# A two-branch recurrent encoder with 32 experts: single-input work goes from VectorE to ScalarE, and the router and the end are rearranged

## The chip, the cores and the metric

The kernel runs on one core of a Trainium2 chip. The metric is the device time of one execution in microseconds (us). Before the change it is 1595.73 us, the median of three runs (1595.01 to 1598.45).

## The reference, cut to what matters

One layer works on 256 tokens of width 1024, in float32.

```
p = x @ w_in                                   # 1024 x 10560
o_a = hgrn2(p...)      # 8 heads, gated linear attention, both directions, chunks
o_b = rwkv7(p...)      # 16 heads, delta-rule recurrence, both directions;
                       # decays, a and g come from low-rank products (64, 64, 128)
merged = sigmoid(gate_a) * (o_a @ proj_a) + sigmoid(gate_b) * (o_b @ proj_b)
x = layernorm(ALPHA * x + merged @ w_out)
logits = x @ router_w + router_b               # top 4 of 32 experts, softmax
h = x[tok] @ w1[e] + b1[e]                     # 1024 -> 2048
act = glu * sigmoid(1.702 * glu) * (lin + 1)   # clamped at 7
y = act @ w2[e] + b2[e]                        # 1024 -> 1024
x = layernorm(ALPHA * x + sum of gate * y)
```

## The kernel before, in words

The program has a front, a router and an expert stage.

**The front** runs four streams that a small loop in the source (`interleave`) mixes by hand-set costs; the order on each engine comes from a scheduler of the language that works by priority. The dense stream loads tiles of `w_in` (512 KB each, through the queue of SP) and multiplies them with the transposed x (L148). The prepare stream (`rwkv_prepare`, one call for each of four groups of heads) makes the operands of the rwkv7 recurrence: a low-rank product (L466, L473), decays, scores `L` (L527, L547), and by `inverse` the inverse of a small triangular matrix `N` (L575, L577), with `Q` its two scaled halves (L581) and, at its end, a clearing of one half of `L` (L607). The run stream (`rwkv_run`) walks eight steps for each group: `step_operand` builds `Z` (L654, L656 and copies from PSUM by `cp`, L96 on ScalarE and L98 on VectorE), `chain` multiplies with `L`, `Y` and `Z` (L679, L690, L704), and `finish` normalises to `yn` (L725), which TensorE transposes (L731). The mix stream (`hgrn_mix`) does the same for the other branch in eight levels with `KK`, `QQ` and `FT` (L778, L821, L871), collects `Am`, and scales `on` (L893). Groups overlap: while group c runs, group c+1 is prepared.

Then the gates, proj_b, proj_a and w_out follow on TensorE, with weights split into two parts of lower precision and three matmuls for each.

**The router.** The last layer-norm's statistics (`deviations`) go to VectorE, the logits' matmuls (L1047) to TensorE. From `lg` VectorE makes the mask `mk` of the four best; TensorE counts positions (L1103 to L1105), VectorE makes the one-hot `oh`, and `pick_tokens` collects each expert's tokens by matmul (L1152).

**The expert stage** runs 32 experts with an order written out by hand for TensorE, VectorE and ScalarE. An expert has 12 tiles of 1 MiB, eight of `w1` (`first`, L1191) and four of `w2` (`second`, L1221). Twenty tiles fit on the chip; a load waits until the tile before it in its place is used. `seq` is the order of loading: for each expert the first LA = 3 tiles of the next one's `w1`, then its own `w2`, then the other five. `scatter` (L1235) adds an expert's result, in a high and a low part `yh` and `yl` (L1226, L1227), to the sums `acc` in PSUM.

After the last expert the program reads the largest count of tokens (L1377) and branches past a block for experts with over 64 tokens; then come the sums of the last layer norm (L1413), its `rsqrt` by Newton steps (L73 to L81), four scalings (L1423 to L1427, on ScalarE, GpSimd and VectorE), four more (L1431) and the stores.

Of the kernel before, what the change touches and what calls it, by code (L numbers as in the profile page):

```python
# [48 lines left out]
def tile_encoder(ctx: ExitStack, tc: tile.TileContext, A, out):  # L49
# [361 lines left out]
    def rwkv_prepare(qi, rw, tmp):  # L411
# [18 lines left out]
        for r in range(2):  # L430
            V.tensor_scalar(k0[:, r], kt[:, r], col(pv, "kk", 2 * qi + r), None, op0=OP.mult)
# [24 lines left out]
        cp(V, vt.rearrange("p t r c -> p (t r c)"), b)  # L456
        yield 1

        def pair(r):
# [13 lines left out]
            T.matmul(b[:, :S], lhsT=aup[:, cj], rhs=lora[:64, 1, :], start=True, stop=True)  # L473
# [77 lines left out]
        def inverse():  # L551
# [28 lines left out]
            for u in range(2):  # L580
                V.tensor_scalar(Q[:, :, 16 * u:16 * u + 16], N, half[:, u:u + 1], None, op0=OP.mult)  # L581
# [24 lines left out]
            for h, d, q in quads:  # L606
                V.memset(L[h][q, d, :, 0:32], 0.0)  # L607
# [8 lines left out]
    def rwkv_run(qi, rw, W):  # L616
# [25 lines left out]
        def step_operand(i):  # L642
# [6 lines left out]
            for h in range(2):  # L649
# [8 lines left out]
                for d in range(2):  # L658
                    cp((V, SC)[d], Zi[rb(h):rb(h) + 64, :, h, d, :], bv[64 * d:64 * d + 64, :, 64 * h:64 * h + 64])
# [87 lines left out]
    def hgrn_in(g, hp):  # L747
# [24 lines left out]
    def hgrn_mix(g, hp):  # L772
# [684 lines left out]
```

## Time and profile before

| | before |
|---|---|
| median of three runs | 1595.73 us |
| the profiled execution, own time | 1598.41 us |
| its span, first to last instruction | 1596.6 us |
| TensorE, VectorE, ScalarE, GpSimd busy | 1456.0, 592.7, 373.4, 95.0 us |
| weights and other data read | 464.48 MB |
| mean granted clock of TensorE | 0.974 |

PE is TensorE's matmuls, PEld its weight loads, DVE VectorE, ACT ScalarE, POOL GpSimd, SP the engine that only issues transfers; a name with q behind it is that engine's queue. Times in the rows are us unless marked ns. A float32 matmul stands in the records as two.

### The profile page before, as it was taken

To read this page: it belongs to the slowest core of one execution; us is meant where nothing else is said; L and a number is where in the kernel's file an instruction comes from. 1 tells how busy PE (TensorE), PEld (TensorE's weight loads), DVE (VectorE), ACT (ScalarE), POOL (GpSimd) and SP (SyncE) were. 2 spreads that over 40 slices of the span, in tenths; PEclk is the share of its full clock that TensorE was granted. 3 is DMA by queue.
4 is the path that set the end of the run, shared out by engine and by line. 5 is a ranking of instruction groups with operands and counts; after the bars stand their busy time and mean duration, and the time that the engine had idled before them with its cause. 6 is when DMAs were issued, how large, how long until landed. Compare 5 with 4: busy or idle time off the path is not lost. (4 is left out here: it accounts for less than half of the span.)

```text
span 1596.6 us, 27102 instructions
## 1 busy us (share of the span) xinstructions
PE 1456.0 (91%) x11323; PEld 798.6 (50%) x11323; DVE 592.7 (37%) x1547; ACT 373.4 (23%) x984; POOL 95.0 (6%) x132
## 2 busy tenths in 40 slices
PE   8989989989879998999999999899999888888884
PEld 7667667667666897444434333244443233323221
DVE  4685985985973475111112111112111111111113
ACT  1426335345325252211111111101111011001000
POOL 0310210211210000000000000000000000000000
PEclk9999999999999998999999999989899999999996
DMA  6322222322334786799999999999999999999993
GB/s 189 107 70 66 85 72 68 98 71 68 106 127 143 274 297 260 302 418 415 418 417 415 418 419 414 418 418 415 418 417 415 417 418 416 417 418 416 416 417 133
DMA packets 133982, 467.36 MB, mean 293 GB/s; under 512 B 9545, under 2 KB 66781, under 8 KB 101085
## 3 DMA queue, kind: packets, MB, share of 16 engines
q1 hardware_dynamic: 129280, 460.88, 74.1%
q10 hardware_dynamic: 4572, 4.68, 0.9%
q8 instruction: 91, 1.49, 0.4%
q14 instruction: 39, 0.31, 0.1%
HBM read 464.48 MB, written 1.05 MB: 292 GB/s over the span
## 5 line engine op out<-in xcount | busy, mean ns | idle before, releaser
L148 PE MATMUL bank_d<-xT,wt 128*128 128x256 f32 x1200 | 310.0, 397 | 0.3 <-DMA wt<-in_w_in_dram 0.3
L148 PEld LDWEIGHTS bank_d<-xT,wt 128*128 128x128 f32 x1200 | 217.1, 193 | 39.6 <-issue 5.8
L1227 DVE SCALAR_TENSOR_TENSOR yl<-ypb,slotg,yh 128x512 fp32r<-128x512 f32 x32 | 24.0, 751 | 491.1 <-ACT yh L1226 491.1
L1191 PE MATMUL hpb<-ring_l,xg 128*64 128x512 f32 x416 | 99.7, 607 | 4.7 <-DMA ring_l<-in_moe_w_dram 4.7
L1173 DVE TENSOR_SCALAR ot<-tpb 128x256 fp32r<-128x256 f32 x32 | 13.6, 425 | 232.0 <-ACT tpb L1172 232.0
L1191 PE MATMUL hpb<-ring_r,xg 128*64 128x512 f32 x400 | 94.4, 598 | 3.3 <-DMA ring_r<-in_moe_w_dram 3.3
L1191 PE MATMUL hpb<-ring_p,xg 128*64 128x512 f32 x400 | 94.5, 598 | 1.7 <-DMA ring_p<-in_moe_w_dram 1.6
L1226 ACT ACTIVATE yh<-ypb,slotg 128x512 fp32r<-128x512 f32 x32 | 22.0, 687 | 309.9 <-PE ypb L1221 309.9
L1152 PE MATMUL tpb<-oh,x 128*128 128x256 f32 (+1 forms) x288 | 66.9, 377 | 4.1 <-ACT xg L1157 3.2
L1152 PEld LDWEIGHTS tpb<-oh,x 128*128 128x128 f32 x288 | 49.6, 197 | 35.6 <-DVE glu L1203 17.9
L1172 ACT ACTIVATE tpb<-tpb 128x256 f32<-128x256 f32 x32 | 11.8, 368 | 234.1 <-PE tpb L1170 230.8
L1138 POOL TENSOR_TENSOR ohg<-oh,gate 128x512 f32<-128x512 f32 (+1 forms) x9 | 8.6, 951 | 867.8 <-PE tpb L1170 853.4
L1191 PEld LDWEIGHTS hpb<-ring_l,xg 128*64 128x64 f32 x416 | 29.3, 140 | 57.8 <-issue 41.2
L1221 PE MATMUL ypb<-ring_p,aT 128*64 128x512 f32 x208 | 48.9, 600 | 8.1 <-DMA ring_p<-in_moe_w_dram 8.1
L1221 PE MATMUL ypb<-ring_l,aT 128*64 128x512 f32 x208 | 50.7, 616 | 5.0 <-DMA ring_l<-in_moe_w_dram 4.8
L1191 PE MATMUL hpb<-ring_b,xg 128*64 128x512 f32 x208 | 50.6, 611 | 4.7 <-DMA ring_b<-in_moe_w_dram 4.7
L1221 PE MATMUL ypb<-ring_r,aT 128*64 128x512 f32 x208 | 49.3, 598 | 5.8 <-DMA ring_r<-in_moe_w_dram 5.8
L1191 PE MATMUL hpb<-ring_q,xg 128*64 128x512 f32 x208 | 49.2, 597 | 5.1 <-DMA ring_q<-in_moe_w_dram 5.1
L1191 PEld LDWEIGHTS hpb<-ring_r,xg 128*64 128x64 f32 x400 | 27.6, 136 | 51.6 <-issue 39.2
L1191 PE MATMUL hpb<-ring_s,xg 128*64 128x512 f32 x208 | 49.2, 598 | 2.2 <-DMA ring_s<-in_moe_w_dram 2.2
L1205 ACT ACTIVATE sgm<-glu 128x256 f32<-128x256 f32 x64 | 26.7, 417 | 104.8 <-DVE glu L1203 104.8
L1191 PEld LDWEIGHTS hpb<-ring_p,xg 128*64 128x64 f32 x400 | 26.9, 136 | 48.5 <-issue 41.0
(329 smaller groups left out, 2211.6 us busy)
## 6 DMA issues: line engine op xcount, KB each, us to landing
ring_l<-in_moe_w_dram SPq DMA_DIRECT2D x78, 1024.0 KB
ring_p<-in_moe_w_dram SPq DMA_DIRECT2D x76, 1024.0 KB
ring_r<-in_moe_w_dram SPq DMA_DIRECT2D x76, 1024.0 KB
wt<-in_w_in_dram SPq DMA_DIRECT2D x84, 512.0 KB
ring_s<-in_moe_w_dram SPq DMA_DIRECT2D x40, 1024.0 KB
ring_e<-in_moe_w_dram SPq DMA_DIRECT2D x38, 1024.0 KB
ring_q<-in_moe_w_dram SPq DMA_DIRECT2D x38, 1024.0 KB
ring_b<-in_moe_w_dram SPq DMA_DIRECT2D x38, 1024.0 KB
```

What stands on the lines that cost most here:

```text
L148: T.matmul(o, lhsT=lhsT, rhs=rhs, start=n == 0, stop=n == last)
L1138: G.tensor_tensor(out=ohg[:, :, :n], in0=oh[:, :, :n], in1=gate[:, :, es[0]:es[0] + n].unsqueeze(3).to_broadcast([P, 2, n, 64]), op=OP.mult)
L1152: T.matmul(b[:, kk * 256:kk * 256 + ne * 64], lhsT=x1[t][:, n * P:(n + 1) * P], rhs=oh[:, t, :ne].rearrange("p e s -> p (e s)"), start=t = ...
L1172: SC.activation(b[:, :S], b[:, :S], AF.Copy, accum_out=sg)
L1173: V.tensor_scalar(ot, b[:, :S], 0.0, None, op0=OP.is_gt)
L1191: T.matmul(self.hbs[cc][64 * j:64 * j + 64, :], lhsT=self.xg[:, k, self.ei, :], rhs=self.w1[k][:, c0:c0 + 512], start=False, stop=k == KT - 1)
L1205: SC.activation(sgm[cc], glu[cc], AF.Sigmoid, scale=1.702)
L1221: T.matmul(yb[64 * j:64 * j + 64, :], lhsT=self.aT[:, k % 4, 64 * (k // 4):64 * (k // 4) + 64], rhs=self.w2[k][:, j * 512:(j + 1) * 512], ...
L1226: SC.activation(yh, yb, AF.Copy, scale=self.sg)
L1227: V.scalar_tensor_tensor(out=yl, in0=yb, scalar=self.sg, in1=yh.bitcast(F32), op0=OP.mult, op1=OP.subtract)
```

## The change

- Ten groups of operations with one input go from VectorE to ScalarE: `k0`, the copy of `vt`, `Q`, the clearing of `L`, the other half of the copies of `Z`, `yn` (with a small product `nb` more), the copy of `hq`, `KK`, four copies into `Am`, and `on`.
- The low-rank weights sit in one tile `ups` with 128 rows, the rows without weights cleared once; the matmuls read all 128 rows.
- In the router four matmuls whose result nobody reads follow the logits, and both halves of `x1` are normalised on ScalarE.
- The last expert's `w1` is loaded whole before the `w2` of the expert before it, and its first layer is computed before that expert's second.
- The read of the largest count moves to expert 4, the sums of the last layer norm (`sums()`, the four bn_stats) stand ahead of the branch and again inside the block, the last `scatter` goes token half by token half.
- In the last layer norm the Newton steps go to GpSimd, and all four first scalings to VectorE.

```
@@ rsqrt(..., pooled=False)
+            if pooled:
+                G.tensor_tensor(out=t, in0=s, in1=y, op=OP.mult)
+                G.tensor_tensor(out=t, in0=t, in1=y, op=OP.mult)
+                G.tensor_scalar(t, t, -0.5, 1.5, op0=OP.mult, op1=OP.add)
+                G.tensor_tensor(out=y, in0=y, in1=t, op=OP.mult)
+                continue
@@ before the streams
+    V.memset(lora[64:128, 1, :], 0.0)
+    ups = fc.tile([P, 3, 256], F32, name="ups")
+    V.memset(ups[64:128, 0:3:2, :], 0.0)
+    V.memset(ups[0:64, 1, :], 0.0)
@@ rwkv_prepare
-        wup = tmp.tile([P, 256], F32, name="wup")
-        nc.scalar.dma_start(out=wup, in_=A["rw_w_up"][0].rearrange("a l n -> (a l) n")[:, cq])
...
+        for d in range(2):
+            nc.scalar.dma_start(out=ups[64 * d:64 * d + 64, d], in_=A["rw_w_up"][0][d][:, cq])
+        nc.scalar.dma_start(out=ups[0:64, 2], in_=A["rw_a_up"][0][:, cq])
...
-            V.tensor_scalar(k0[:, r], kt[:, r], col(pv, "kk", 2 * qi + r), None, op0=OP.mult)
+            SC.activation(k0[:, r], kt[:, r], AF.Copy, scale=col(pv, "kk", 2 * qi + r))
...
-        cp(V, vt.rearrange("p t r c -> p (t r c)"), b)
+        cp(SC, vt.rearrange("p t r c -> p (t r c)"), b)
...
+                T.matmul(b[:, d * S:(d + 1) * S], lhsT=ups[:, d, cj], rhs=lora[:, 0, :], start=True, stop=True)
...
-                V.tensor_scalar(Q[:, :, 16 * u:16 * u + 16], N, half[:, u:u + 1], None, op0=OP.mult)
+                SC.activation(Q[:, :, 16 * u:16 * u + 16], N, AF.Copy, scale=half[:, u:u + 1])
...
-                V.memset(L[h][q, d, :, 0:32], 0.0)
+                SC.activation(L[h][q, d, :, 0:32], ident[q, 0:1].unsqueeze(2).to_broadcast([32, 16, 32]), AF.Copy, scale=0.0)
@@ rwkv_run
-                    cp((V, SC)[d], Zi[rb(h):rb(h) + 64, :, h, d, :], bv[64 * d:64 * d + 64, :, 64 * h:64 * h + 64])
+                    cp(SC, Zi[rb(h):rb(h) + 64, :, h, d, :], bv[64 * d:64 * d + 64, :, 64 * h:64 * h + 64])
...
-                V.tensor_scalar(ynv[:, n, :], yg[:, n, :], mv[:, n, 0:1], rs[:, n:n + 1],
-                                op0=OP.subtract, op1=OP.mult)
+                SC.activation(ynv[:, n, :], yg[:, n, :], AF.Identity, scale=rs[:, n:n + 1], bias=nb[:, n:n + 1])
@@ hgrn_in, hgrn_mix
-        cp(V, q, b)
+        cp(SC, q, b)
...
-        V.tensor_scalar(KK[:, ::-1, :], FT, -1.0, 1.0, op0=OP.mult, op1=OP.add)
+        SC.activation(KK[:, ::-1, :], FT, AF.Identity, scale=-1.0, bias=ones[:, 0:1])
...
-                        cp(V, Am[r0, sh_, :, c0:c0 + 64], bv[r0, :, sh_, :])
+                        cp(SC, Am[r0, sh_, :, c0:c0 + 64], bv[r0, :, sh_, :])
...
-            V.tensor_scalar(on[:, a, :], ov[:, a, :], rs[:, a:a + 1], None, op0=OP.mult)
+            SC.activation(on[:, a, :], ov[:, a, :], AF.Copy, scale=rs[:, a:a + 1])
@@ order of loading
-        seq += nxt[:LA] + [(e, n) for n in range(KT, 12)] + nxt[LA:]
+        la = KT if e == NE - 2 else LA
+        seq += nxt[:la] + [(e, n) for n in range(KT, 12)] + nxt[la:]
@@ router
+        b = bc()
+        for n in range(4):
+            T.matmul(b, lhsT=ident, rhs=xT.rearrange("p k s -> p (k s)"), start=True, stop=True)
...
-        SC.activation(x1[1], x1[1], AF.Identity, scale=sd[:, 1:2], bias=nb[:, 1:2])
-        V.tensor_scalar(x1[0], x1[0], mv[:, 0, 0:1], sd[:, 0:1], op0=OP.subtract, op1=OP.mult)
+        for t in range(2):
+            SC.activation(x1[t], x1[t], AF.Identity, scale=sd[:, t:t + 1], bias=nb[:, t:t + 1])
@@ expert loop and the end
+            if e == 4:
+                most = nc.values_load(cnti[0:1, 0:1], min_val=0, max_val=S)
...
+            if e + 1 == NE - 1:
+                break
             prev.second()
-        prev.scatter(acc, False, True)
-    most = nc.values_load(cnti[0:1, 0:1], min_val=0, max_val=S)
+        last = cur
+        last.first([3, 4])
+        last.first([5])
+        last.places(ohg)
+        last.first([6, 7])
+        last.activate()
+        prev.second()
+        last.transpose()
+        prev.scatter(acc, False, False)
+        last.second()
+        last.scatter(acc, False, True)
...
+        sums()
     with tc.If(most > 64):
...
-    for c in range(2):
-        SC.activation(f[1][c], acc[1][c], AF.Identity, bias=nm[:, 1:2])
-        G.tensor_tensor(out=f[1][c], in0=f[1][c], in1=fin[:, 0, cols[c]], op=OP.mult)
-    sd = rsqrt(mo, mv[:, :, 1], 2, 1.0, 1e-5)
+        sd = rsqrt(mo, mv[:, :, 1], 2, 1.0, 1e-5, pooled=True)
...
+        for t in range(2):
+            for c in range(2):
+                V.scalar_tensor_tensor(out=f[t][c], in0=acc[t][c], scalar=nm[:, t:t + 1], in1=fin[:, 0, cols[c]],
+                                       op0=OP.add, op1=OP.mult)
```

## Rows read from the trace of the kernel before

**Rows 1.** The page, memory rate in 40 equal slices of the span.

```profile
GB/s 189 107 70 66 85 72 68 98 71 68 106 127 143 274 297 260 302 418 415 418 417 415 418 419 414 418 418 415 418 417 415 417 418 416 417 418 416 416 417 133
```

**Rows 2.** Windows, sums: 80-120, 160-240, 280-360, 400-480; then 120-160, 240-280, 360-400, 500-600.

```profile
sum 280.00, PE 241.19 PEld 184.71 DVE 244.77 ACT 96.27 POOL 52.96; mean PE 60.30 PEld 46.18 DVE 61.19 ACT 24.07 POOL 13.24
...
sum 220.00, PE 219.06 PEld 176.56 DVE 116.11 ACT 105.86 POOL 11.49; mean PE 54.76 PEld 44.14 DVE 29.03 ACT 26.47 POOL 2.87
```

**Rows 3.** Waits of PE, 0 to 640 us: total, times, longest.

```profile
PE bank_h L821 <- DVE As L823: 6.7, 2, 3.3
...
PE bank_p L446 <- DVE nw_y L81: 0.3, 1, 0.3
```

**Rows 4.** Timeline, router: start, duration, instruction, idle before it and releaser.

```profile
631.50 0.81 DVE L1060 TENSOR_SCALAR x<-x,ln_mv,nw_y 128x1024 f32<-128x1024 f32 x1
...
634.15 0.61 PE L1103 MATMUL tpb<-mk,tri 128*128 128x32 f32 x2 [3.74 <-issue]
...
639.56 2.08 PE L1152 MATMUL tpb<-oh,x 128*128 128x128 f32 x8 [0.96 <-ACT xg L1157]
...
642.42 3.17 PE L1191 MATMUL hpb<-ring_l,xg 128*64 128x512 f32 x10
...
645.21 2.04 SPq L933 DMA_DIRECT2D ring_l<-in_moe_w_dram  x2
```

**Rows 5.** Window 640 to 645 us: busy of engines, granted clock, DMA share, GB/s.

```profile
640.00:645.00 5.00, 5.00 (x22) 2.50 (x21) 0.00 (x0) 0.81 (x2) 0.00 (x0) 0.59 0.00 0
```

**Rows 6.** Window 1570 to 1571 us.

```profile
1570.00:1571.00 1.00, 1.00 (x6) 0.28 (x4) 0.00 (x0) 0.00 (x0) 0.00 (x0) 0.50 0.06 25
```

**Rows 7.** Timeline, the last experts and the end.

```profile
1547.77 1.94 PE L1221 MATMUL ypb<-ring_p,aT 128*64 128x512 f32 x8 [0.60 <-DMA ring_p<-in_moe_w_dram]
...
1574.18 3.65 PE L1221 MATMUL ypb<-ring_s,aT 128*64 128x512 f32 x16
...
1578.65 0.75 DVE L1227 SCALAR_TENSOR_TENSOR yl<-ypb,slotg,yh 128x512 fp32r<-128x512 f32 x1 [11.19 <-ACT yh L1226]
...
1579.46 0.73 PE L1235 MATMUL acc<-yl,ot 64*128 64x512 f32 x4
1582.83 2.49 DVE L1413 BATCH_NORM_STATS2 ln_st<-acc 128x6 f32<-128x512 f32 x4 [3.43 <-DVEq L1377]
...
1589.17 0.16 DVE L80 SCALAR_TENSOR_TENSOR nw_t<-nw_t,nw_y 128x2 f32<-128x2 f32 x1
...
1590.82 2.74 DVE L1431 SCALAR_TENSOR_TENSOR x<-x,nw_y,fin 128x512 f32<-128x512 f32 x4
```

**Rows 8.** Groups of DVE, 0 to 640 us: count, busy us, mean ns, idle before.

```profile
L98 DVE COPY Z<-bank_c 64x128 f32<-64x128 f32 x56 | 15.8, 282 | 21.4 <-PE bank_c L648 13.5 <-ACT Z L96 7.3
...
L778 DVE TENSOR_SCALAR KK<-FT 128x1024 f32<-128x1024 f32 x4 | 2.7, 687 | 0.0
...
L98 DVE COPY hq<-bank_d 128x512 f32<-128x512 f32 x4 | 2.7, 676 | 0.0
```

**Rows 9.** Groups of ACT, 0 to 640 us.

```profile
L654 ACT ACTIVATE Z<-id,scl 64x64 f32<-64x64 f32 x112 | 33.3, 337 | 10.1 <-PE bank_c L731 9.2
...
L96 ACT ACTIVATE Z<-bank_c 64x128 f32<-64x128 f32 x56 | 15.0, 270 | 24.0 <-DVE Z L98 23.1
...
L1059 ACT ACTIVATE x<-x,ln_nb,nw_y 128x1024 f32<-128x1024 f32 x1 | 1.2, 1240 | 2.3 <-DVE ln_nb L985 2.3
```

**Rows 10.** Groups of PE, 0 to 640 us.

```profile
L466 PE MATMUL bank_p<-lora,wup 64*128 64x256 f32 x32 | 11.1, 428 | 0.0
...
L485 PE MATMUL bank_p<-sqb,blk 128*128 128x256 f32 x16 | 5.1, 402 | 1.1 <-DVE sqb L482 0.9
```

**Rows 11.** Instructions of L1377 on VectorE's queue: ns min, median, max, start.

```profile
L1377 DVEq COMPARE_BRANCH  x1: 72/72/72, 1579.8 to 1579.8; - x1
```

**Rows 12.** Groups of POOL, whole span.

```profile
L875 POOL TENSOR_TENSOR FT<-FT 128x16 f32<-128x16 f32 x4 | 1.5, 364 | 1.0 <-DVE N L577 0.8
```

**Rows 13.** Waits of ACT, 0 to 530 us.

```profile
ACT bias L285 <- DMA BK<-in_moe_b_dram: 23.9, 4, 8.3
```

More of the change, by code (lines that the diff above doesn't have):

```diff
@@ L472, in pair @@
             b = bs()
[L473 removed]
+            T.matmul(b[:, :S], lhsT=ups[:, 2, cj], rhs=lora[:, 1, :], start=True, stop=True)
             sigmoid(at, b[:, :S], col(hm, "a0", j))
@@ L721, in finish @@
             rs = rsqrt(rw, mv[:, :, 1], 8, 1.0, 64e-5)
+            nb = rw.tile([P, 8], F32, name="gn_nb")
+            V.scalar_tensor_tensor(out=nb, in0=mv[:, :, 0], scalar=-1.0, in1=rs, op0=OP.mult, op1=OP.mult)
             yn = rw.tile([P, 4, P], F32, name="yn", tag="Z", bufs=3)
@@ L1230, in scatter @@
         def scatter(self, acc, first, last):
-            for n, y in enumerate(self.y):
-                for t in range(2):
-                    for j in range(2):
-                        T.matmul(acc[t][j], lhsT=self.ot[64 * j:64 * j + 64, t * P:(t + 1) * P],
-                                 rhs=y[64 * j:64 * j + 64, :], start=first and n == 0, stop=last and n == 1)
+            for n, t, j in ([(n, t, j) for t in range(2) for n in range(2) for j in range(2)] if last else
+                            [(n, t, j) for n in range(2) for t in range(2) for j in range(2)]):
+                T.matmul(acc[t][j], lhsT=self.ot[64 * j:64 * j + 64, t * P:(t + 1) * P],
+                         rhs=self.y[n][64 * j:64 * j + 64, :], start=first and n == 0, stop=last and n == 1)
     def bias_parts(e):
@@ L1408, in tile_encoder @@
                 V.tensor_copy(acc[t][j], fin[:, t, j * 512:(j + 1) * 512])
+        sums()
         gains2()
-    st = mo.tile([P, 2, 2, 6], F32, name="ln_st2")
-    for c in range(2):
+    osrc = out[0].rearrange("(t p) d -> p t d", p=P)
+    with tc.manual_schedule(engines={mybir.EngineType.DVE}):
+        mv = mo.tile([P, 2, 2], F32, name="ln_mv2")
         for t in range(2):
-            V.bn_stats(st[:, t, c, :], acc[t][c])
-    osrc = out[0].rearrange("(t p) d -> p t d", p=P)
-    mv = mo.tile([P, 2, 2], F32, name="ln_mv2")
@@ L1416, in tile_encoder @@
-    for t in range(2):
-        V.bn_aggr(mv[:, t, :], st[:, t].rearrange("p a b -> p (a b)"))
-    nm = mo.tile([P, 2], F32, name="ln_nm")
-    V.tensor_scalar(nm, mv[:, :, 0], -1.0, None, op0=OP.mult)
-    f = [[x1[t][:, c * 512:(c + 1) * 512] for c in range(2)] for t in range(2)]
-    cols = [slice(c * 512, c * 512 + 512) for c in range(2)]
-    for c in range(2):
-        SC.activation(f[1][c], acc[1][c], AF.Identity, bias=nm[:, 1:2])
-        G.tensor_tensor(out=f[1][c], in0=f[1][c], in1=fin[:, 0, cols[c]], op=OP.mult)
@@ new lines, in tile_encoder @@
+        f = [[x1[t][:, c * 512:(c + 1) * 512] for c in range(2)] for t in range(2)]
+        cols = [slice(c * 512, c * 512 + 512) for c in range(2)]
+        sd = rsqrt(mo, mv[:, :, 1], 2, 1.0, 1e-5, pooled=True)
+        nm = mo.tile([P, 2], F32, name="ln_nm")
+        V.tensor_scalar(nm, mv[:, :, 0], -1.0, None, op0=OP.mult)
+        for t in range(2):
+            for c in range(2):
+                V.scalar_tensor_tensor(out=f[t][c], in0=acc[t][c], scalar=nm[:, t:t + 1], in1=fin[:, 0, cols[c]],
+                                       op0=OP.add, op1=OP.mult)
@@ L1436 @@
+        for t in range(2):
+            for c in range(2):
+                V.scalar_tensor_tensor(out=f[t][c], in0=f[t][c], scalar=sd[:, t:t + 1], in1=fin[:, 1, cols[c]],
+                                       op0=OP.mult, op1=OP.add)
+                (nc.sync, nc.scalar)[t].dma_start(out=osrc[:, t, cols[c]], in_=f[t][c])
 _INS = ['x', 'w_in', 'hg_lb_logits', 'hg_norm_w', 'rw_mu', 'rw_w0', 'rw_w_up', 'rw_a0', 'rw_a_up', 'rw_g_up',
```

18 lines of the change are left out of this document (5 added, 13 removed).

## The prediction

> **What bounds the kernel now.** I read the page first: the slices of the DMA rate, then stretches of busy time by engine, then who waits for whom, and last the timeline of two short places. The slices split the program in two [rows 1]. From the eighteenth slice on, about 680 us, the memory moves 414 to 419 GB/s without a break: the expert weights. Before that it moves far less. The expert stage is therefore a fixed load at a fixed rate. Its length does not change; what changes is when it starts, and what is left to do after its last byte.
>
> The start hangs on the front. There TensorE is full in three stretches of 40 us and again from 500 to 600 us. Between them lie four stretches, 280 us in all, in which VectorE is busy 244.8 us and TensorE only 241.2 us, so 38.8 us of TensorE lie idle [rows 2]. In the table of waits, twelve rows of recurrence matmuls name a VectorE operation as the releaser; they sum to 33.0 us, and the first and last of them are shown [rows 3]. So VectorE is the longer engine there, but not by much: TensorE is 86% busy in the same time.
>
> At the router, memory stands still. The 20 weight tiles that fit are all loaded, and the next is issued at 645.21 us, after the first expert's first matmuls have freed a tile [rows 4]. From 640 to 645 us the rate is 0 and TensorE's granted clock 0.59 [rows 5], so mostly at the lower of its two levels (1.2 and 2.4 GHz). TensorE had been idle 3.74 us just before its first router matmul [rows 4].
>
> At the end the last bytes land at about 1571 us, when 25 GB/s are left, with the clock at 0.50 [rows 6]. TensorE works on until 1577.8 us (1574.18 and 3.65), VectorE begins its sums at 1582.83 us and ends at 1593.56 us [rows 7].
>
> **The change, part by part.**
>
> *Ten operations from VectorE to ScalarE.* VectorE loses ten groups of instructions, from the copies of Z with 15.8 us to that of hq with 2.7; they sum to 57.6 us [rows 8]. ScalarE gains more than that. A copy of 64x128 takes it 270 ns, a scaled one of 64 columns 337 ns, one of 1024 columns 1240 ns [rows 9]. With a straight line between the last two for the widths in between, the ten groups cost it 68 us, an estimate. In the four stretches ScalarE is busy 96 of 280 us [rows 2], so even if two thirds of the 68 us fall there it is half full.
> What is that worth? The ceiling is TensorE's idle time, 38.8 us. VectorE's work in the four stretches, 244.8 us, would fall by about a sixth (57.6 of the 361 us that the stretches of rows 2 hold together), again 39 us. The floor is nothing: the stretches are as much TensorE's as VectorE's, and each hand-over to ScalarE adds a wait. Of the waits, only those on yn (4.3 us), on the clearing of L (1.2 us) and on KK (0.6 us) name a moved operation; the other 27 us can shrink only because VectorE comes to its other work sooner. A quarter of those and all of the 6.1 us make 13 us, a third of the ceiling: **-13 us**, bounds -39 and 0. Everything behind moves up with it, since TensorE is full from 500 to 600 us and the expert stage follows.
> The Trainium skill, page "ScalarE: Activation LUTs", section on rules for kernel authors, says to give add, multiply and the like to VectorE, not ScalarE. The trace agrees for a single operation: KK's 687 ns against 1240 ns for that width. By the rule the move would cost 68 minus 57.6, some 10 us; by the stretches it does not, because ScalarE has the room.
>
> *Low-rank weights at 128 rows.* The matmuls keep their count and their 256 columns; a matmul half takes 428 ns with 64 rows, and 402 ns in another matmul with 128 [rows 10]. Three clearings at the start lie beside the first dense tiles, below 1 us, and one more DMA issue for each of four groups stands in ScalarE's queue, far ahead of its use. I put nothing for it; uncovered it would be 2 us.
>
> *Router.* Four matmuls of 128x512 are added between the logits and the router's own first matmul, into the 3.74 us in which TensorE waits for VectorE. At full clock a tile of four such matmuls (eight records, half as wide a stationary side) takes 1.94 us [rows 7], so four cost 1.9 to 3.9 us: they fit. At half clock they take up to 7.8 us and hold the router's matmul by up to 4 us. In return the clock may stay up. From 634.15 to 645.21 us I add the TensorE work at the low clock: three groups of 0.61, two picks of 2.08, and 2.5 for the first weight tile (eight of the ten records in 3.17), 8.5 us; at full clock half of it goes, 4.2 us. VectorE also no longer normalises x1[0] (0.81 us [rows 4]) ahead of the logits, since ScalarE does both halves; the gates that wait for ScalarE's exponential come later, but beside TensorE's first matmuls. Sum -5 at best; the four matmuls start with the clock about to fall, which may cost 1 us: **-4 us**, bounds -5 and +3. The memory stands still here, so this moves the whole expert stage; behind it memory is late again, with 2.5 us for a tile of 1 MiB at 418 GB/s against TensorE's 1.94 us.
>
> *The end.* The last expert's first weights now come before the second weights of the expert before it, so that only second-layer work is behind the last byte. A second-layer tile takes 1.94 us at full clock, and TensorE waits for memory tile by tile there. The last byte at 1571 us and one tile give 1573 against 1577.8 us: -4.9 us. If the clock has fallen, as it has now, the last tile takes 3.9 us, and two before it lag: -2. I take -4.
> VectorE's sums (2.49 us) move ahead of the branch, the register load to expert 4. What stays is the time from VectorE's branch at 1579.8 us [rows 11] to its next work at 1582.83 us, 3.0 us. Today that runs while TensorE finishes; then it stands behind the sums. yl ends at 1579.40 us; the scatter adds 0.8, the sums 2.49, the branch 3.0: 6.3 us, where now it is 5.9 (3.43 and 2.49). +0.4. Were the 3.0 us a load of the register, which moves, it would be -2.6; I keep that as the bound. The load itself, now for expert 4, waits for counts that are made at expert 2; behind it stand, on SP's queue, loads for 20 tiles further on, and on TensorE matmuls that run ahead of memory, so I put nothing for it, at most 1 us.
> The Trainium skill, page "Runtime: NRT & Kernel Launch", section on instruction fetch mechanics, says that a taken branch to a page not at hand stalls on a fetch. The trace agrees so far that the branch itself is 72 ns of the 3.0 us; by the rule the stall moves with the branch, as in the sum above, and by the other reading it goes.
> From the end of its sums VectorE now takes 8.2 us (1585.32 to 1593.56). Then: six small operations 1.1, four wide ones 2.74, and four more 2.74, 6.6 us, if GpSimd's twelve small steps are done by then. They are bounded by 0.16 us (VectorE's own) and 0.364 us each (GpSimd's 128x16 [rows 12]): 1.9 to 4.4 us plus hand-overs, against the 2.9 us that cover them. -1.6 to 0; I take -1.
> End together: **-4.6 us**, bounds -9 and -1.6.
>
> Sum: 13 + 4 + 4.6 = 21.6 us off the profiled execution's own 1598.4 us (span 1596.6, 1.8 around it): 1576.8. That execution lies 2.7 us above the median of the runs shown, 1595.73, so the median would be 1574; I say **1575 us**.
>
> **Rivals.**
> *A, the forecast:* 1566 to 1586 us. Chance 0.53.
> *B, the front does not get shorter.* VectorE's work goes, but TensorE, 86% busy and strictly in order, refills the time, or each hand-over returns the gain. For it: few waits name a moved operation. Against: VectorE is over 87% busy across the stretches. Left are 4 and 4.6: 1598.4 - 8.6 - 2.7 = 1587 us. Chance 0.2.
> *C, the front gives most of its ceiling,* because the clearing of L and the two half-width scalings sit in the last group's inverse, where no dense tile is left to fill TensorE. Three quarters of 39 is 29: 1558 us. Chance 0.16.
> *D, slower.* ScalarE's queue is in order, and it stands four times, 23.9 us in all, for the bias rows of the experts from memory [rows 13]. Copies that now run on VectorE would stand behind those waits, and the last recurrence behind the copies. If all of it reached TensorE, 23.9 against 8.6 saved: 1598.4 + 15.3 - 2.7 = 1611; half of it gives 1599. It decides once more than 12 us reach TensorE with nothing gained in the front. Against: these waits lie where gate tiles keep TensorE full. Chance 0.08. The skill's rule on ScalarE leads to the same side.
> *E, the added matmuls run at the low clock and hold the router* (+3 in place of -4): 1582 us, inside A. Chance 0.03.
>
> **How the numbers follow.** About 0.2% (3 us) is what a measurement of this kernel can tell from no change. A, C, E and nearly all of B are faster by more, together 0.89; same 0.04 is B with a poor end or D with a small wait; slower 0.07 is the rest of D. The range that leaves out no more than 2 in 10 reaches from C's 1558 to B's 1587 with a poor end, 1590.
>
> **What would show it.** Right: in the four stretches VectorE's busy time falls by about 40 us and TensorE's idle with it; the proj matmuls begin some 13 us earlier; the rate of 0 at the router shrinks from about 7 us to about 3, at a clock of 1.0 in TensorE's first expert tiles; the last matmul ends within 3 us of the last byte; a gap of about 3 us follows the sums. Wrong: ScalarE near full in those stretches with TensorE waiting for it, half-clock matmuls at the router, or a break in the 415 GB/s.

## The result and the profile after

The changed kernel takes **1608.48 us** (median of five, 1604.65 to 1611.39) against 1595.73: ratio **1.0075, 95% interval 1.0059 to 1.0091**. It is slower by about 0.75%; 1575 us was forecast. The profiled execution is the fastest of the five (1604.65 us, span 1602.9). One execution of a test kernel (e20) took 4949.7 us where its others took 1599 to 1606; it is in no ratio.

Where the time went is read from the issue of three loads on SP's queue and from the end of the span. The first proj_b load starts at 557.26 us instead of 540.17, the first weight load behind the router at 658.14 instead of 645.21 [rows 4], and the span ends at 1602.9 instead of 1596.6. So the front costs +17.1 us, and everything behind it gives 10.8 back: the router 3.8 (from the issue of ring_q to that of ring_l 14.27 us, before 18.04), the end 6.6 (from ring_l to the last instruction 944.8 us, before 951.4), the rest 0.4.

SP's queue before, then the kernel after: SP's queue, TensorE and VectorE at the end.

```profile
540.17 5.12 SPq L131 DMA_DIRECT2D wt<-in_proj_b_dram  x2
...
627.17 0.82 SPq L933 DMA_DIRECT2D ring_q<-in_moe_w_dram  x2
```

```profile
557.26 5.12 SPq L137 DMA_DIRECT2D wt<-in_proj_b_dram  x2
...
643.87 0.82 SPq L942 DMA_DIRECT2D ring_q<-in_moe_w_dram  x2
...
658.14 2.04 SPq L942 DMA_DIRECT2D ring_l<-in_moe_w_dram  x2
...
1584.97 1.94 PE L1235 MATMUL ypb<-ring_s,aT 128*64 128x512 f32 x8 [0.29 <-SPq L1412]
...
1589.03 2.49 DVE L1406 BATCH_NORM_STATS2 ln_st<-acc 128x6 f32<-128x512 f32 x4 [0.59 <-PE acc L1248]
...
1592.56 0.28 DVE L1450 BATCH_NORM_AGGREGATE ln_mv<-ln_st 128x2 f32<-128x12 f32 x2 [1.03 <-DVEq L1412]
...
1596.80 2.74 DVE L1462 SCALAR_TENSOR_TENSOR x<-x,nw_y,fin 128x512 f32<-128x512 f32 x4 [0.42 <-POOL nw_y L83]
```

In the windows of [rows 2] VectorE is relieved, but TensorE is no fuller. The line is that of the four stretches that VectorE bound. The windows are fixed in time while the program runs some 2 to 10 us later in them, so they do not hold quite the same work as before; a stretch that goes by the program follows with the experiments.

```profile
sum 280.00, PE 235.83 PEld 181.41 DVE 225.04 ACT 131.93 POOL 51.87; mean PE 58.96 PEld 45.35 DVE 56.26 ACT 32.98 POOL 12.97
```

ScalarE is busy 132 of 280 us, so it has the room that the forecast gave it. TensorE's waits have changed hands: from 10 to 560 us it stands 29.3 us for VectorE (33.0 before, [rows 3]) and 22 us for ScalarE (7.9 before). The longest wait of TensorE for ScalarE after, and one of ScalarE's own in the same stretch:

```profile
PE bank_c L687 <- ACT L L615: 7.9, 1, 7.9
```

```profile
ACT bias L291 <- DMA BK<-in_moe_b_dram: 22.3, 4, 9.2
```

The costs of three moved operations on ScalarE after (count, busy us, mean ns, idle before):

```profile
L615 ACT ACTIVATE L<-ident 32x512 f32<-32x512 f32 x16 | 10.0, 626 | 7.0 <-PE bank_p L600 6.7
L735 ACT ACTIVATE yn<-bank_y,gn_nb,nw_y 128x64 f32<-128x64 f32 x32 | 9.9, 415 | 32.4 <-DVE gn_nb L731 32.4
...
L787 ACT ACTIVATE KK<-FT,ones 128x1024 f32<-128x1024 f32 x4 | 4.6, 1158 | 0.0
```

Two places stand out. At the end of a run ScalarE stops 9.3 us for `gn_nb`, which VectorE makes behind the next group's preparation; behind yn in the queue stand the next mix's last gate FT and its KK. Whether that reaches TensorE is a question for the experiments. Timeline after, third run, ScalarE:

```profile
435.14 2.47 ACT L735 ACTIVATE yn<-bank_y,gn_nb,nw_y 128x64 f32<-128x64 f32 x8 [9.32 <-DVE gn_nb L731]
437.47 0.64 ACT L764 ACTIVATE FT<-bank_d 128x512 f32<-128x512 f32 x1
...
439.40 1.17 ACT L787 ACTIVATE KK<-FT,ones 128x1024 f32<-128x1024 f32 x1
```

In the last group ScalarE stops 7.45 us for the experts' bias rows (BK), with the clearing of L behind it, and TensorE stands 7.90 us for L. L is not the only thing behind that wait: VectorE, which splits the same rows, stands for ScalarE's copy until 473.86 us (7.51 us), right ahead of its last RS at 474.74. The loads of those rows are issued from ScalarE's own queue, and they are issued later than before. After, last group:

```profile
445.45 0.63 ACTq L289 DMA_DIRECT2D BK<-in_moe_b_dram  x1
...
458.74 0.54 ACTq L289 DMA_DIRECT2D BK<-in_moe_b_dram  x1
...
472.99 0.84 ACT L291 ACTIVATE bias<-BK 128x768 bf16<-128x768 f32 x1 [7.45 <-DMA BK<-in_moe_b_dram]
473.85 2.55 ACT L615 ACTIVATE L<-ident 32x512 f32<-32x512 f32 x4
...
474.53 0.42 PE L687 MATMUL bank_c<-W,L 128*32 128x64 f32 x2 [7.90 <-ACT L L615]
```

Before, the same loads stood at 426.15 and 442.00 us, and the second wait ended in the middle of the inverse. It was not free there either: VectorE stood 3.27 us behind it, and TensorE 4.03 us for KS, which ScalarE made right after the rows' copy:

```profile
426.15 0.63 ACTq L283 DMA_DIRECT2D BK<-in_moe_b_dram  x1
...
442.00 1.13 ACTq L283 DMA_DIRECT2D BK<-in_moe_b_dram  x2
449.79 0.84 ACT L285 ACTIVATE bias<-BK 128x768 bf16<-128x768 f32 x1 [8.08 <-DMA BK<-in_moe_b_dram]
...
450.66 0.96 DVE L286 TENSOR_TENSOR BK<-BK,bias 128x768 f32<-128x768 f32 x1 [3.27 <-ACT bias L285]
...
451.20 0.66 PE L821 MATMUL bank_h<-QQ,KS 128*32 128x32 f32 x32 [4.03 <-ACT KS L96]
```

### The profile page after: what moved, and what is told of

Read it like the earlier page. It is cut to its first block, busy times and chain, and to the rows that moved or that the text cites. A ratio compares the mean times of both kernels' runs of the same rounds, so it can differ in the third digit from the quotient of the medians.

```text
span 1602.9 us, 27153 instructions
## 1 busy us (share of the span) xinstructions
PE 1456.7 (91%) x11331; PEld 802.4 (50%) x11331; DVE 549.2 (34%) x1382; ACT 432.9 (27%) x1147; POOL 88.7 (6%) x142
## 5 line engine op out<-in xcount | busy, mean ns | idle before, releaser
L154 PE MATMUL bank_d<-xT,wt 128*128 128x256 f32 x1200 | 313.8, 399 | 0.1
L1205 PE MATMUL hpb<-ring_p,xg 128*64 128x512 f32 x416 | 98.4, 598 | 2.3 <-DMA ring_p<-in_moe_w_dram 2.2
L1229 ACT ACTIVATE aT<-tpb 128x512 f32<-128x512 f32 x32 | 19.1, 597 | 122.4 <-PE tpb L1228 122.4
L1235 PE MATMUL ypb<-ring_p,aT 128*64 128x512 f32 x192 | 45.0, 599 | 6.8 <-DMA ring_p<-in_moe_w_dram 6.8
```

Source lines behind the costliest of these rows:

```text
L154: T.matmul(o, lhsT=lhsT, rhs=rhs, start=n == 0, stop=n == last)
L1205: T.matmul(self.hbs[cc][64 * j:64 * j + 64, :], lhsT=self.xg[:, k, self.ei, :], rhs=self.w1[k][:, c0:c0 + 512], start=False, stop=k == KT - 1)
L1229: SC.activation(self.aT.rearrange("p c s -> p (c s)"), b, AF.Copy)
L1235: T.matmul(yb[64 * j:64 * j + 64, :], lhsT=self.aT[:, k % 4, 64 * (k // 4):64 * (k // 4) + 64], rhs=self.w2[k][:, j * 512:(j + 1) * 512], ...
```

## The experiments

Eighteen kernels were run. The table gives fourteen of them (e6, e7, e8 and e12 stand in the text): the median, the ratio to runs of the kernel before taken beside it (medians 1595.5 to 1598.0) with the 95% interval, and three lengths from the trace: from VectorE's first RS (end of the first inverse) to the first bn_stats of the last run (`gn_st`); of that the two middle groups (from the first run's `gn_st` to the third's); and the last group (to the fourth's). The rows of RS and `gn_st` behind the first of these lengths are shown further down for four kernels.

| kernel | us | ratio, interval | RS to end of runs | middle two | last |
|---|---|---|---|---|---|
| before | 1595.7 | | 417.9 | 231.1 | 126.5 |
| after | 1608.5 | 1.0075, 1.0059 to 1.0091 | 436.6 | 239.6 | 133.3 |
| e5 ten moves alone | 1614.4 | 1.0113, 1.0088 to 1.0138 | 437.8 | 244.0 | 129.7 |
| e1 all ten back | 1587.2 | 0.9938, 0.9918 to 0.9957 | 417.4 | 230.9 | 125.5 |
| e2 mix's four back | 1593.6 | 0.9962, 0.9946 to 0.9978 | 429.2 | 227.5 | 133.4 |
| e3 Z, yn, L back | 1584.6 | 0.9913, 0.9890 to 0.9937 | 413.7 | 232.4 | 120.9 |
| e4 preparation's three back | 1594.5 | 0.9970, 0.9956 to 0.9984 | 428.3 | 237.2 | 127.1 |
| e13 yn back | 1589.0 | 0.9940, 0.9918 to 0.9962 | 417.2 | 231.0 | 122.6 |
| e14 L back | 1606.4 | 1.0053, 1.0034 to 1.0072 | 436.1 | 237.1 | 133.9 |
| e15 before, yn alone moved | 1593.8 | 0.9983, 0.9968 to 0.9997 | 416.0 | 230.4 | 124.8 |
| e9 rows split on GpSimd | 1603.1 | 1.0033, 1.0018 to 1.0048 | 431.3 | 237.6 | 130.1 |
| e10 hon behind W | 1606.3 | 1.0047, 1.0032 to 1.0063 | 438.9 | 240.5 | 135.2 |
| e16 yn's inputs on GpSimd | 1601.9 | 1.0036, 1.0022 to 1.0049 | 430.0 | 239.4 | 126.8 |
| e18 yn behind KK | 1601.0 | 1.0028, 1.0012 to 1.0044 | 426.8 | 233.5 | 129.5 |
| e19 rows loaded early | 1613.2 | 1.0115, 1.0094 to 1.0135 | 426.6 | 242.4 | 120.3 |
| e20 rows early, yn behind KK | 1602.6 | 1.0043, 1.0027 to 1.0060 | 416.8 | 233.5 | 117.8 |

By these marks the front's +17.1 us are -1.6 ahead of the first RS, +3.4 from there to the first `gn_st` (60.3 before, 63.7 after), +8.5 in the middle groups and +6.8 in the last. Each length comes from one trace. Among five kernels without any of the ten moves (before, e1, e6, e7, e8) the columns spread by 2.6, 1.9 and 3.3 us.

### Which part of the change

e1: the ten moves undone in the kernel after, all else kept. e5: the ten moves alone on the kernel before.

```diff
-            SC.activation(k0[:, r], kt[:, r], AF.Copy, scale=col(pv, "kk", 2 * qi + r))
+            V.tensor_scalar(k0[:, r], kt[:, r], col(pv, "kk", 2 * qi + r), None, op0=OP.mult)
...
```

> The changed kernel with all ten operations back on VectorE; low-rank weights, router and end stay changed. Theory 1 (the moved operations make the front longer): the +17 us of the front go, -3.8 at the router and -6.6 at the end stay, 1585 us (1582 to 1590), proj_b loads begin near 540 us. Rival (the 128-row low-rank weights, or another order of the other instructions, make the front longer): 1600 us or more, proj_b loads near 557 us.

> The kernel before with the ten moves alone. Theory 1: the front costs +17 us and nothing gives it back, 1613 us (1608 to 1618). Rival (low-rank or order): within 3 us of 1596. If the moves and the low-rank weights each carry a part: 1600 to 1607.

Measured: 1587.2 and 1614.4 us. The moves make the front longer, by some 20 us (1608.5 less 1587.2; 1614.4 less 1595.7), and nothing else does.

e8 and e6: the low-rank weights alone, and the router's changes alone, on the kernel before; e7: the joined end alone.

```diff
+            T.matmul(b[:, d * S:(d + 1) * S], lhsT=ups[:, d, cj], rhs=lora[:, 0, :], start=True, stop=True)   # e8
...
+            T.matmul(b, lhsT=ident, rhs=xT.rearrange("p k s -> p (k s)"), start=True, stop=True)              # e6
...
+        prev.scatter(acc, False, False)                                                                       # e7
+        last.second()
```

> The kernel before with the 128-row low-rank weights alone. Theory 1: nothing, 1596 us within 3. Rival: +10 to +17 us, 1606 to 1613, because ScalarE issues one more load for each group and the matmuls take twice the rows.

> The kernel before with the four added matmuls and the normalising of both halves on ScalarE alone. By the two profiles the router is worth -3.8 us: 1592 us (1590 to 1594), clock 1.0 from 627 to 645 us. If what the router gives is lost in the expert stage, which memory limits: 1596 within 2.

> The kernel before with the joined end alone. The forecast's term is -4.6 us: 1592 to 1593 us. By the two profiles the stretch from the first weight load behind the router to the end is 6.6 us shorter: 1590 to 1591. If the end is bound by memory and the rest is lost elsewhere: 1597.

Measured: low-rank 1594.6 us (0.9987, 0.9973 to 1.0000), next to nothing; router 1593.6 us (0.9994, 0.9974 to 1.0014), not to be told from no change; end 1589.9 us (0.9957, 0.9940 to 0.9973), -6.9 us. Its interval is 4.3 to 9.6 us, so the forecast's 4.6 lies inside it.

For the router the traces say more than the times. From ring_q to ring_l the five kernels without its change take 17.5 to 18.7 us. Of the fifteen with it five take 14.3 us (after among them), nine 15.9 to 16.0 (e6 among them), one 17.6. The instructions are the same; the granted clock is not. The last stretch of the router, first after, then e6, with the second group of picks:

```profile
655.00:658.10 3.10, 3.10 (x22) 1.62 (x22) 0.00 (x0) 0.81 (x2) 0.00 (x0) 1.00 0.13 56
...
647.00 3.68 PE L1062 MATMUL bank_c<-xT,ident 128*128 128x512 f32 x8
...
654.67 1.16 PE L1166 MATMUL tpb<-oh,x 128*128 128x128 f32 x8 [0.96 <-ACT xg L1171]
```

```profile
636.00:640.00 4.00, 4.00 (x18) 1.66 (x18) 0.00 (x0) 0.81 (x2) 0.00 (x0) 0.67 0.00 0
...
634.88 1.79 PE L1156 MATMUL tpb<-oh,x 128*128 128x128 f32 x8 [0.96 <-ACT xg L1161]
```

### Which of the moves

e2, e3 and e4 take back the mix's four moves (hq, KK, Am, on), the run's three (Z, yn, L), and the preparation's three (k0, vt, Q), by the same lines in reverse. Theory 1 holds ScalarE's queue responsible, where what waits stops all behind it; theory 2 ScalarE's busy time.

```diff
-        SC.activation(KK[:, ::-1, :], FT, AF.Identity, scale=-1.0, bias=ones[:, 0:1])
+        V.tensor_scalar(KK[:, ::-1, :], FT, -1.0, 1.0, op0=OP.mult, op1=OP.add)                 # e2, and hq, Am, on
-                SC.activation(L[h][q, d, :, 0:32], ident[q, 0:1]..., AF.Copy, scale=0.0)
+                V.memset(L[h][q, d, :, 0:32], 0.0)                                              # e3, and Z, yn
```

> The changed kernel with the mix's four moves (hq, KK, Am, on) back on VectorE, the other six left on ScalarE. Theory 1 (the order of ScalarE's queue: evictions of the mix, which wait there for their matmuls, stand ahead of the run chain's copies of W): about half of the 20 us come back, 1597 to 1600 us. Theory 2 (ScalarE's added busy time itself): 15.1 of the 59.2 us go, a quarter of 20 us, 1602 to 1604.

> The changed kernel with Z, yn and the clearing of L back on VectorE, the other seven left on ScalarE. Theory 1: the clearing of L goes out from behind ScalarE's wait for the bias rows (TensorE's wait of 7.9 us), and yn from ahead of other copies: 8 to 11 us come back, 1596 to 1600. Theory 2 (busy time): 35.1 of 59.2 us go, 12 of 20 us, 1595 to 1598, and TensorE's waits fall in all four groups alike.

> The changed kernel with the preparation's three moves (k0, vt, Q) back on VectorE, the other seven left on ScalarE. Theory 1: nothing stands in front of the chain through these, 1606 to 1609 us. Theory 2 (busy time): 9 of 59.2 us go, 3 us, 1604 to 1606.

Measured: 1593.6, 1584.6, 1594.5 us: 15, 24 and 14 of the 21 us come back. All three are more than either theory allowed. The parts do not add up, so something works only when several moves stand together. e3 beats both kernels.

e13 and e14 take back one move each; e10 forces one order on ScalarE; e9 takes ScalarE's wait for the bias rows away from it.

```diff
+                V.tensor_scalar(ynv[:, n, :], yg[:, n, :], mv[:, n, 0:1], rs[:, n:n + 1], op0=OP.subtract, op1=OP.mult)   # e13
+                V.memset(L[h][q, d, :, 0:32], 0.0)                                                                       # e14
+        with tc.issue_after(box[f"w{g}"].ins):        # e10: w is the run's first copy of W
+            SC.activation(on[:, a, :], ov[:, a, :], AF.Square, accum_out=ms[:, a:a + 1])
+        G.tensor_copy(bg, fg)                         # e9, in place of ScalarE's two copies
```

> The changed kernel with only yn back on VectorE. Theory 1b (ScalarE stands 32.4 us in four waits for yn's inputs, with the next group's copies behind it): 1595 to 1600 us, that is 9 to 13 us back. Theory 2 (busy time): 9.9 of 59.2 us go, 3 us back, 1604 to 1607.

> The changed kernel with only the clearing of L back on VectorE. Theory 1b (it goes out from behind ScalarE's wait for the bias rows, 7.9 us of TensorE's time in the last group; and with it the order of the run's W ahead of hon comes back in two groups): 1596 to 1601 us. Theory 2 (busy time): 10.0 of 59.2 us go, 3 us back, 1604 to 1607.

> The changed kernel with all ten moves, and one order forced: the mix's squares (hon), which wait on ScalarE for the mix's last matmuls, are issued behind the run's first copy of W instead of ahead of it. Work and engines are the same. Theory 1a (the place of hon decides): 1596 to 1602 us. Theory 1b (the order matters, but hon's place is not the place that decides; the version with Z, yn and L back also has hon ahead of W): 1606 to 1610. Theory 2 (busy time): 1606 to 1610.

> The changed kernel, all ten moves on ScalarE, with the two copies of the experts' bias rows on GpSimd, so that ScalarE never waits for those rows (22.3 us in four waits before). Theory 1 with rival D's wait as a cause: the last group's wait for L (7.9 us) and for W (2.9 us) go, 1598 to 1602 us. If ScalarE's wait for the bias rows costs nothing that would not be lost behind it anyway: 1606 to 1609.

Measured: 1589.0, 1606.4, 1606.3 and 1603.1 us. Theory 2 falls here: yn and L take the same busy time off ScalarE (9.9 and 10.0 us), and one gives 19.5 us, the other 2. Forcing the place of hon gave next to nothing. Undoing L and moving the rows' copies give 2 and 5 us, and the rows show that the wait stays: in e14 VectorE stands 7.32 us ahead of RS, as it did in the kernel after (7.51 us); in e9 GpSimd waits 12.99 us for the load and VectorE 7.90 us behind it. VectorE of e14; GpSimd and VectorE of e9:

```profile
472.97 0.96 DVE L292 TENSOR_TENSOR BK<-BK,bias 128x768 f32<-128x768 f32 x1 [7.32 <-ACT bias L291]
473.85 0.68 DVE L603 TENSOR_TENSOR RS<-bank_p,m 128x512 f32<-128x512 f32 x1
```

```profile
470.80 0.82 POOL L291 CAST bias<-BK 128x768 bf16<-128x768 f32 x1 [12.99 <-DMA BK<-in_moe_b_dram]
...
471.65 0.96 DVE L292 TENSOR_TENSOR BK<-BK,bias 128x768 f32<-128x768 f32 x1 [7.90 <-POOL bias L291]
```

### What it is about yn

e15 moves yn alone; e16 makes its inputs on GpSimd; e18 leaves all on the same engines and issues yn behind KK of the next group (in the source the end of a run then waits until that KK has been issued). In the expectations theory 1b is that ScalarE stands at yn with the next mix's FT, Z and KK behind it.

```diff
+            rs = rsqrt(rw, mv[:, :, 1], 8, 1.0, 64e-5, pooled=True)      # e16, and nb by two operations of GpSimd
...
+            if qi < 3:
+                yield ("need", f"kk{qi + 1}")                            # e18
+            with tc.issue_after(box[f"kk{min(qi + 1, 3)}"].ins):
+                SC.activation(ynv[:, n, :], yg[:, n, :], AF.Identity, scale=rs[:, n:n + 1], bias=nb[:, n:n + 1])
```

> The kernel before with yn alone moved to ScalarE (with its nb on VectorE); 9.9 of the 59.2 us of ScalarE's new work. Theory 1b (ScalarE stands at yn until VectorE, behind the next group's preparation, has made nb; FT, Z and KK of the next mix stand behind it): 1606 to 1615 us. Theory 2 (busy time): 3 us, 1598 to 1601. Theory 3 (yn costs only beside the other moves): 1596 to 1602.

> The changed kernel with all ten moves on ScalarE, but the Newton steps for yn's scale and its nb on GpSimd, so that they no longer stand behind the next group's preparation on VectorE. ScalarE's busy time is the same. Theory 1b: ScalarE's waits at yn (9.3, 9.3, 9.3 and 4.4 us) fall below 4 us each, and 1588 to 1597 us. Theory 2 (busy time of ScalarE): 1605 to 1610; VectorE loses some 40 small operations in each group, which is worth at most 3 us.

> The changed kernel with all ten moves on the same engines, and one order forced: yn of a group is issued on ScalarE behind KK of the next group, so that the next mix's gates and KK no longer stand behind it. Theory 1b: 1588 to 1598 us. Theory 2: 1605 to 1610. If the order made for the rest suffers from the forced place (Z of the next run behind yn): 1598 to 1605.

Measured: 1593.8, 1601.9 and 1601.0 us. Alone, yn costs nothing, though ScalarE stands 32.8 us for it there as well; KK and the other moved operations are then on VectorE. With yn behind KK the middle two groups take 233.5 us instead of 239.6. ScalarE of e18:

```profile
430.50 0.60 ACT L767 ACTIVATE FT<-bank_d 128x512 f32<-128x512 f32 x1 [9.70 <-PE bank_d L154]
...
432.25 1.15 ACT L790 ACTIVATE KK<-FT,ones 128x1024 f32<-128x1024 f32 x1
433.31 1.57 ACT L738 ACTIVATE yn<-bank_y,gn_nb,nw_y 128x64 f32<-128x64 f32 x5
```

The gain does not come from an earlier KK as such. Counted from the `gn_st` ahead of it (406.59 us before, 416.88 after, 408.73 in e13, 411.86 in e18), KK starts at 28.2 us before, 22.5 after, 21.6 in e13 and 20.4 in e18. So the change made KK earlier, not later, and e13, which gives 8.6 us back in the middle two groups, moves it by 0.9 us a group. Nor is the 9.3 us for which ScalarE stands a measure of the loss: in e18 it stands 9.70 us at the same place, for FT's own matmul. Nothing in TensorE's waits in these groups names FT or KK. KK before, then in e13:

```profile
434.76 0.69 DVE L778 TENSOR_SCALAR KK<-FT 128x1024 f32<-128x1024 f32 x1
```

```profile
430.34 1.15 ACT L786 ACTIVATE KK<-FT,ones 128x1024 f32<-128x1024 f32 x1
```

What the traces do show is TensorE's time over the same 3008 matmul records of the two groups: 212.1 us busy and 19.0 idle before, 215.0 and 24.6 after, 211.4 and 19.6 in e13, 210.7 and 22.8 in e18. Of the 6.1 us that e18 gains, 4.2 are thus busy time at a higher granted clock. How yn's place leads there is open, and so is whether the clock has another cause. The second of the two groups, after and e18:

```profile
295.35:416.88 121.53, 108.96 (x1504) 82.27 (x1503) 79.44 (x206) 65.31 (x197) 18.05 (x27) 0.94 0.26 74
```

```profile
295.06:411.86 116.80, 105.58 (x1504) 80.39 (x1503) 78.65 (x206) 65.36 (x197) 18.33 (x27) 0.99 0.26 77
```

e16 got its time elsewhere: yn still waits 4.5 us, the middle two groups stay at 239.4, but the wait for the bias rows ahead of the last RS is down to 4.36 us (last group 126.8).

The table now splits cleanly. The middle two groups take 237 us or more in every kernel that has both yn and KK on ScalarE with yn in front (after, e4, e5, e9, e10, e14, e16, e19), and at most 233.5 in all others. The last group takes 129 us or more in the seven kernels in which a wait of over 6 us for the bias rows ends within 2.5 us ahead of the last RS (after, e2, e5, e9, e10, e14, e18), and at most 127.1 in all others. That is theory 4, two causes in different groups; the table fits it and does not prove it. The limits of both splits were drawn with the table in hand: in e13 and e16 a wait for the rows also ends 1.75 us ahead of the last RS, but it is 3.93 and 4.36 us long.

### The rows loaded early, alone and with yn behind KK

e19 loads the bias rows in tiles of their own, long before they are split; e20 adds e18's order. All ten moves stay on ScalarE.

```diff
+        fg = rows[g] = rw.tile([P, 768], F32, name=f"rows{g}")
...
+            if c == 1:
+                for g in range(4):
+                    load_biases(rw, g)
```

> The changed kernel, all ten moves on ScalarE, with the four loads of the experts' bias rows issued in the second group into tiles of their own, so that neither ScalarE nor VectorE waits for them in the last group. Theory 4 (two causes, each in its own groups: yn ahead of the next mix's KK on ScalarE costs 8 us in groups 1 and 2; the wait for the bias rows ahead of the last group's L costs 7): 1600 to 1603 us, the last group's two stages fall from 133 to about 126 us, groups 1 and 2 stay at 238 to 241. If the last group's loss has another cause: 1606 to 1609, last group 131 to 135.

> The same with yn of a group issued on ScalarE behind KK of the next group: both causes of theory 4 taken away, all ten moves still on ScalarE, its busy time unchanged. Theory 4: 1592 to 1597 us, groups 1 and 2 at 232 to 235 us, the last group at 124 to 128. If ScalarE's busy time or each hand-over costs: 1600 to 1606. If the moves then also give what the forecast priced (13 us): below 1585.

Measured: 1613.2 and 1602.6 us; both totals miss. The scheduler put the eight loads at the very start of the program, and the splitting behind them too: ScalarE's eight copies (6.5 us) and VectorE's eight subtractions (7.6 us) run from 28 to 48 us instead of 453 to 516. The first inverse ends 16.6 to 16.8 us later. ScalarE's queue and its first copies in e20, then the same copies in the kernel after:

```profile
13.96 12.50 ACTq L290 DMA_DIRECT2D rows<-in_moe_b_dram  x8
...
L295 ACT ACTIVATE bias<-rows x4: 832/842/843, 27.8 to 41.7; 128x768 bf16<-128x768 f32 x4
```

```profile
L291 ACT ACTIVATE bias<-BK x4: 842/842/843, 453.2 to 510.1; 128x768 bf16<-128x768 f32 x4
```

So these two kernels do not take the wait away with the work left in place. From the first RS to the end of the runs they are without the splitting, and their last groups, 120.3 and 117.8 us, lie below the 126.5 of the kernel before, which waited for these rows itself. How much of the 10.0 us of e19 is the wait, no run separates; a kernel before with the rows early was not run.

e18 and e13 hold the same work in that stretch as the kernel after (943 matmul records of dense tiles in each; before it is 931). First RS and last `gn_st` on VectorE, in this order: before, after, e18, e13.

```profile
115.18 0.69 DVE L595 TENSOR_TENSOR RS<-bank_p,m 128x512 f32<-128x512 f32 x1
533.08 1.15 DVE L717 BATCH_NORM_STATS2 gn_st<-bank_y 128x6 f32<-128x64 f32 x8 [1.63 <-PE bank_y L638]
```

```profile
113.61 0.69 DVE L603 TENSOR_TENSOR RS<-bank_p,m 128x512 f32<-128x512 f32 x1 [1.19 <-PE bank_p L600]
550.18 1.15 DVE L725 BATCH_NORM_STATS2 gn_st<-bank_y 128x6 f32<-128x64 f32 x8 [1.64 <-PE bank_y L646]
```

```profile
114.50 0.69 DVE L603 TENSOR_TENSOR RS<-bank_p,m 128x512 f32<-128x512 f32 x1 [0.99 <-PE bank_p L600]
541.32 1.15 DVE L725 BATCH_NORM_STATS2 gn_st<-bank_y 128x6 f32<-128x64 f32 x8 [1.63 <-PE bank_y L646]
```

```profile
114.20 0.69 DVE L603 TENSOR_TENSOR RS<-bank_p,m 128x512 f32<-128x512 f32 x1 [0.99 <-PE bank_p L600]
531.37 1.15 DVE L725 BATCH_NORM_STATS2 gn_st<-bank_y 128x6 f32<-128x64 f32 x8 [1.63 <-PE bank_y L646]
```

The differences are 417.9 us before, 436.6 after, 426.8 with yn behind KK, 417.2 with yn back on VectorE, and 416.8 with the rows early and yn behind KK. Of the 18.7 us the place of yn among ScalarE's operations gives 9.8 back, and yn's return to VectorE all of it, with nine moves still on ScalarE. In e13 the first of the rows' loads is issued at 425.92 us again, and the wait ahead of the last RS shrinks with it. That the stretch of e20 is as long as before is a sum of unlike parts: 5.2 us more to the first `gn_st`, 2.4 more in the middle groups, 8.7 less in the last. TensorE is idle 36.3 us in the stretch before, 48.3 after, 35.8 in e13. Before, after, e13:

```profile
115.20:533.10 417.90, 381.60 (x5327) 286.67 (x5326) 294.63 (x801) 179.98 (x545) 63.30 (x89) 0.98 0.32 95
```

```profile
113.60:550.20 436.60, 388.32 (x5337) 294.28 (x5338) 257.38 (x666) 230.85 (x684) 59.08 (x89) 0.95 0.31 91
```

```profile
114.20:531.40 417.20, 381.37 (x5337) 289.62 (x5337) 260.21 (x687) 224.55 (x660) 60.70 (x89) 0.98 0.31 95
```

e12 is e3 with the bias rows' copies on GpSimd.

> The changed kernel with Z, yn and the clearing of L back on VectorE and the two copies of the bias rows on GpSimd. With Z, yn and L back it takes 1584.6 us. If ScalarE's waits for the bias rows still cost in the last group: 1579 to 1583. If they are covered there: 1583 to 1586.

Measured: 1584.7 us (0.9921, 0.9907 to 0.9935): no better than e3. These two are the fastest kernels of the study; e1 (1587.2) lies 2.6 us above with overlapping intervals, so a gain from the seven moves kept in e3 is not shown.

## Why the prediction was wrong

**The ten operations.** Forecast -13 us, with 0 as the upper bound; the trace shows +17.1, the runs some +20. The prices were near: ScalarE's busy time grew by 59.5 us (432.9 against 373.4), priced at 68. The rule quoted from the Trainium skill (page "ScalarE: Activation LUTs", rules for kernel authors) pointed to the right side, and KK takes 1158 ns against 687 [rows 8], but the busy time is not what cost: e13 and e14 relieve ScalarE alike and lie 17 us apart. The step that failed is the sentence that ScalarE has the room. It had room on average, 132 of 280 us busy, but an average says nothing of an engine that takes its instructions in a fixed order. With yn in that order beside the other nine moves the front is some 20 us longer; with yn back on VectorE and the nine kept it is as long as before. In the last group the clearing of L stood behind a wait for memory, and TensorE stood 7.90 us for it. In the middle groups, 8.5 us longer, yn's place is shown to matter, but how its cost reaches TensorE stays open, as does the +3.4 us ahead of them.

*Rival D* named the mechanism of the last group, put 1599 to 1611 us to it and got 0.08. The measured time lies in its range, but in part by luck: the last group is 6.8 of the front's 17.1 us, and the rest no rival saw. D fell to the sentence that those waits "lie where gate tiles keep TensorE full". That did not hold even before: in the second of the four waits TensorE is busy 4.24 of 8.08 us, and 4.03 us, up to 451.20, it stood for KS behind that wait. Nor do the waits stay where they were: ScalarE issues the loads itself, and they moved by 19.3 and 16.7 us (426.15 to 445.45, 442.00 to 458.74), while the last inverse began only 9.1 us later. TensorE in the second wait, before:

```profile
441.71:449.79 8.08, 4.24 (x50) 3.09 (x48) 5.53 (x18) 0.00 (x1) 0.61 (x1) 0.99 0.52 159
```

*The gain* that was to stand against it is not there either. In e13 VectorE is relieved by 34.4 us over the stretch (260.2 against 294.6; the fixed windows of [rows 2] show 20 where 39 were forecast), yet TensorE's idle time is 35.8 against 36.3 us and the stretch 417.2 against 417.9; the whole kernel, 1589.0 us, is no faster than e1 with all moves back (1587.2). So the waits that name no moved operation did not shrink by the quarter that was counted on: rival B, once yn is back.

**Low-rank weights.** Forecast 0; -1.7 us with an interval that reaches 1.0000. Right.

**Router.** Forecast -4 with bounds -5 and +3: -3.8 in the trace after, the added matmuls take 3.68 us (1.9 to 3.9 was said), and the rate's gap shrinks as described. But in ten of the fifteen kernels with the change the stretch is 1.6 us longer or more, in e6 with the clock fallen in its last part, and the term is nearer to -2.

**End.** Forecast -4.6; -6.6 in the trace, -6.9 alone. The trace of before is the longest of its kind here: from the first load behind the router to the end the five kernels without the change take 946.4 to 951.4 us, the fifteen with it 943.1 to 946.1, 4.4 less on average, as forecast. Counted from the first load behind the router, the last second layer ends 3.9 us earlier (said: 4). In the trace after the mis-sized part is the branch: +0.4 was said, with -2.6 as the bound if the gap were the register's load. From the last second-layer matmul to the end of the sums it is 4.6 us instead of 7.5, -2.9, and behind the sums only 1.03 us is left at the branch. The rule of the Trainium skill (page "Runtime: NRT & Kernel Launch", instruction fetch mechanics) would have moved all of the 3.0 us with the branch; the trace leaves it at most this 1.03. From the sums on, 8.0 us against 8.2: without that gap the norm is 1.2 us shorter (said: 1).

Behind the front 10.4 us came off where 8.6 were forecast; the front gave +17.1 in place of -13. That difference of 30 us is most of the 33.5 us between 1575 and 1608.48. The profiled execution also lies 3.8 us below its median, where the forecast had it 1.8 above.

## What to carry to other kernels

An operation that moves to an emptier engine takes a place in that engine's queue: before its duration, ask when its inputs are ready, what stands behind it, and which transfers that queue issues. If taking back any of several moves returns most of the loss, look for an order that they make together, and split the time by stages of the program; totals of versions with different orders do not add. Test a cause by removing it with the work left in place, and look whether the work did stay: e18 changed an order, but e19 and e20 moved the splitting along with its loads, and their shorter stretch proves little. And before a long wait is called the cause, see what its engine does without it: ScalarE's 9.3 us for yn's input became 9.70 us for FT's.

## What the runs showed of the hardware

The same router instructions ran at a granted clock of 1.00 in the kernel after and at 0.67 in the last stretch of e6, 1.16 against 1.79 us for the same eight matmul records. The 1504 records of a middle group took 108.96 us of TensorE at 0.94 and 105.58 at 0.99. Why the clock stays in one and falls in the other, no run tells. Eight small loads put at the start of the program took 12.50 us of ScalarE's queue; with them and the work that came along, the first inverse ended 16.6 us later.
